# Expert stages of a two-layer network: weights in longer runs, the next pair's gather inside this pair's chain, the overflow branch at the end

## The chip, the cores and the metric

The kernel runs on one core of one Trainium2 chip. The metric is device time in microseconds (us) of one execution, taken as the median of the runs.

## What is computed

A stack of two blocks over 256 tokens of 1024 features, all in float32. The first block (two layers of a feed-forward net, three attention branches and another feed-forward net) is not touched. The second block has two layers; each is a mixer (a state space mixer in layer 0, dilated attention in layer 1), a layer norm, a mixture of experts, and a layer norm:

```python
g_w, g_idx = lax.top_k(softmax(xf @ w_rg + b_rg), 1)        # one of 4 groups
e_w, e_idx = lax.top_k(softmax(e_logits of that group), 2)  # two of its 8 experts
gates = g_w * e_w / sum(e_w)
# every expert's tokens, in blocks:
h = silu(xb @ w_gate[e]) * (xb @ w_up[e])                   # 1024 -> 512
y = h @ w_down[e]                                           # 512 -> 1024
x = layer_norm(ALPHA * x + sum over a token's experts of gate * y)
```

There are 32 experts; each one's three matrices hold 2 MiB each, so a layer reads 192 MiB of expert weights.

## The kernel before

**Shape of an expert stage.** `moe` works on x with features on partitions (X["h"] and X["l"], its high and low parts, and X["T"], the sum of both). The router multiplies x with the router's weights (L1302, L1303), turns the logits over to tokens (L1308) and picks experts on VectorE. Meanwhile x is turned to tokens on partitions (L1349, evicted by ScalarE into `xt`, L1350). A product of masks with a triangle gives each token's place in its experts' lists (L1355 to L1359), `rk`.

**A pair.** The 32 experts are worked off as 16 pairs, 64 places to an expert, so that a pair fills 128 columns. `pair(q)` asks for the pair's twelve tiles of weights (`load`, each 1 MiB: four of w_gate, four of w_up, four of w_down), builds the one-hot matrices of places (`ot`, L1580) and the same with the tokens' weights (`ogt`, L1587), and calls `run`. In `run` TensorE does in this order:

1. the gather: `xg` = the pair's tokens as columns, 16 products of 128x128 (L1455) into two PSUM tiles of 512 columns, each copied to SBUF by VectorE (L1460);
2. two transposes of `ogt` (L1463), evicted by ScalarE to `og` (L1465);
3. the gate and up products (L1478) into `gps` and `ups`; ScalarE then makes tanh of `gps` (L188), VectorE two steps to `t` (L1493, L1494);
4. four transposes of `t` into `htp` (L1497), copied by VectorE to `hT` (L1499);
5. the down products (L1510) into two `yp`, evicted by ScalarE to `y` (L1519);
6. eight products of `y` with `og` (L1535), summed over all pairs in `eacc`, four PSUM tiles.

The float32 products are two TensorE instructions each. The stationary side of the gate, up and down products is 64 columns wide, the two experts of the pair side by side; that of the others is 128 wide. The small PSUM tiles (`xgp`, `ogp`, `htp`, `yp`) all come from one pool with two buffers, `mp`, in turn.

In the first pair the term ALPHA * x is added to `eacc` as 16 products of `xt` with a scaled identity (`residual`, L1437), tied behind the gate products. In the last pair `run` also makes the mean of the sum for the layer norm that follows.

**Weights.** SyncE issues the loads. The tiles lie in 21 slots that are used in a fixed turn (`ORDER`, `next_tile`), so the loads run ahead of TensorE by at most that many. Each load sends row `c * 128 + p` of a stretch of the matrix to partition p, column group c:

```python
t = next_tile([128, 4, HID])
x = nc.sync.dma_start(out=t, in_=w[k][h * 512:(h + 1) * 512, :].rearrange("(c p) m -> p c m", p=128))
```

so a contiguous run is one row: 2 KB of w_gate and w_up, 4 KB of w_down.

**Overflow.** An expert may have more than 64 tokens. `beyond` (after pair 1) counts the blocks beyond the first; `more` (after pair 10, `MOREQ`) reads that number into a register of each engine and holds a branch (L1594) around a loop that treats one block a turn. Its body asks for six weight slots of its own, so the turn of slots moves on by six there. With the inputs used the number is zero: the branch is taken past the loop.

The order on each engine is made by a scheduler from the program's order, its dependencies and some ties written by hand.

Of the kernel before, what the change touches and what calls it, by code (L numbers as in the profile page):

```python
# [10 lines left out]
F32 = mybir.dt.float32  # L11
# [7 lines left out]
D = 1024  # L19
S = 256  # L20
KC = D // 128
# [10 lines left out]
W1 = 0  # L32
W2 = 4
# [14 lines left out]
def tile_stack(ctx: ExitStack, tc: tile.TileContext, a: dict, out: bass.AP):  # L48
# [20 lines left out]
    def after_norm(*ins):  # L69
        """no split but the first few between the operations of a layer norm."""  # L70
# [119 lines left out]
    def table(name):  # L190
        """the functions' tables, loaded behind the last tanh."""
# [4 lines left out]
    def warm(out, n, after):  # L196
        """the array's clock falls in a pause: idle products, into a sum not in use, keep it up."""
# [5 lines left out]
    def last_chunks(accs, ks, first):  # L203
        """the products of the last chunks, (wh, wl, mh, ml) each, into one output chunk."""
# [113 lines left out]
    def ffn(l, w1, w2, g, b, setup=None):  # L318
        with pool(name="accps", bufs=1, space=PSUM) as aps, pool(name="gups", bufs=2, space=PSUM) as gps, \
# [26 lines left out]
            def gate_up(js):  # L346
                """the hidden chunks js; features outermost, so that it can start on the first of them."""
# [42 lines left out]
    def log1p_exp_neg_abs(pool, x, shape, tag):  # L390
        """log(1 + exp(-|x|)) by the series of atanh."""
# [34 lines left out]
    def bias_tile(pool, h, queue=None, bufs=3):  # L426
        """T[q, k] = rel[bucket(128 + q - k), h], with the mask of the head's kind."""
# [48 lines left out]
    def token_mix(l):  # L476
        w_in, w_gate, w_out = a["w_in"][l], a["w_gate"][l], a["w_out"][l]
        with ExitStack() as st:
# [25 lines left out]
            def split_pair(t0, t1, c0):  # L504
                """stationary columns: 64 of t0, 64 of t1."""
# [19 lines left out]
            def k_pad(ps, kz, i):  # L525
                """a projected pair of keys into two tiles, each with zeros in the other's rows."""
# [10 lines left out]
            def v_tok(ps, v, i):  # L537
                """keys on partitions: v[:, tile, i, :]."""
# [7 lines left out]
            # compressed keys and values  # L546
# [28 lines left out]
            def compress(i, ts):  # L575
                """four products side by side, then their sum."""
# [26 lines left out]
            # compressed keys  # L603
# [23 lines left out]
            # compressed values  # L627
# [15 lines left out]
            # gates of the three branches and the forget gate  # L643
# [15 lines left out]
            # the running sums of the forget gates  # L659
# [9 lines left out]
            # attention over the compressed blocks, all heads at once  # L669
# [29 lines left out]
            def attend(q, kz, bias, sink=None, gate=None):  # L699
                """probabilities of one head, keys on partitions: [k0 x (q0 q1) | k1 x q1]."""  # L700
# [27 lines left out]
            def pv(po, jobs):  # L728
                """jobs[g]: list of (v of tile 0, v of tile 1 or None, probabilities)."""
# [55 lines left out]
            # NSA  # L785
# [17 lines left out]
            # sliding window with sinks  # L803
# [20 lines left out]
            # forgetting attention  # L824
# [79 lines left out]
    def rsqrt_tile(pool, v, eps, n=S):  # L904
        """(v + eps) ** -0.5, refined by a step of Newton's."""
# [9 lines left out]
    def ssd(g, b):  # L915
        w_in, w_out = a["ssd_w_in_2"][0], a["ssd_w_out_2"][0]
        with ExitStack() as st:
# [13 lines left out]
            def conv(ps, c, dst):  # L931
                """causal convolution of four taps, then twice its silu."""
# [9 lines left out]
            # the keys and queries of the states, B and C  # L942
# [6 lines left out]
            # steps, decays and their running sums  # L949
# [47 lines left out]
            def mix(j, xs, csb, y):  # L997
                """the states' sums for two heads."""
# [115 lines left out]
            # sin, with its sign by row, and cos, one where nothing turns  # L1114
# [136 lines left out]
    NE, CAP, HID, NOV = 32, 64, 512, 7  # L1251
    AHEAD = 7
    MOREQ = 10
# [18 lines left out]
    def router_parts(rp, l):  # L1272
        """the router's weights, high and low parts side by side."""
# [5 lines left out]
    def moe(l, g_, b_, rs, write=False):  # L1279
        w_g, w_u, w_d = a["moe_w_gate_2"][l], a["moe_w_up_2"][l], a["moe_w_down_2"][l]  # L1280
        with ExitStack() as st:
# [27 lines left out]
            warm(accs[0][:, 0, :], W1, x)  # L1309
            # the groups' logits, filled up to eight, then the experts'  # L1310
# [7 lines left out]
            def top(x, name):  # L1318
                """the eight highest logits in order, and where they stand."""
# [8 lines left out]
            # the experts of the other groups far below  # L1328
# [8 lines left out]
            # which experts  # L1337
# [22 lines left out]
            warm(accs[0][:, 0, :], W2, x)  # L1360
# [367 lines left out]
```

## Time and profile before

| | |
|---|---|
| median of 3 runs | 2939.51 us (2937.55 to 2939.96) |
| span of the profiled execution, first to last instruction | 2939.3 us |
| TensorE (products) busy | 2802.7 us, 95% of the span |
| TensorE's weight loads | 2199.8 us, 75% |
| VectorE | 1421.7 us, 48% |
| ScalarE | 1050.9 us, 36% |
| GpSimd | 196.5 us, 7% |
| mean granted TensorE clock | 0.988 |
| moved by DMA | 697.44 MB, mean 237 GB/s |

The profile gives each instruction's start and length, and for each idle stretch the event that ended it. Products are pipelined on TensorE: a row's length includes the way through the array, so rows overlap, and the step between two starts is what one costs. The expert stage of layer 0 runs from about 1684 to 2204 us, that of layer 1 from about 2405 us to the end.

### The profile page before, as it was taken

The page shows a single profiled execution, that of the slowest core. Times are in us where ns is not written, and L with a number is a line of the kernel's source. Part 1 is how long each engine was busy: PE and PEld are TensorE (multiplying, and loading weights), DVE is VectorE, ACT ScalarE, POOL GpSimd, SP SyncE. Part 2 cuts the span into 40 slices and gives each one's busy share as a digit, 9 for nine tenths or more (in the row PEclk, how much of TensorE's full clock was granted, in tenths as well). Part 3 has the DMA queues.
Part 4 walks back from the last instruction along what each step waited for, and adds up shares of the span by engine and source line. Part 5 has one row for each costly group of instructions (what it writes and reads, how often), then busy time and mean ns, then how long its engine had stood idle before and what let it go on. Part 6 is the DMA issues. An engine that isn't in the chain of part 4 may idle for free. (4 is left out here: it accounts for less than half of the span.)

```text
span 2939.3 us, 46679 instructions
## 1 busy us (share of the span) xinstructions
PE 2802.7 (95%) x19161; PEld 2199.8 (75%) x19161; DVE 1421.7 (48%) x3075; ACT 1050.9 (36%) x1949; POOL 196.5 (7%) x263
## 2 busy tenths in 40 slices
PE   8899999999999999999999999999998989999998
PEld 8798899999999889999989854454448974444454
DVE  5466665755655765665688731111127762111113
ACT  4344555544544454544477510000015530000002
POOL 2102000200201100020100100000001010000000
PEclk9899999999999999999999999999999999999999
DMA  8666454455454745445455699998985479999896
GB/s 223 193 201 158 126 159 138 156 184 185 149 194 137 186 130 167 153 139 193 131 194 180 229 364 393 395 393 323 393 305 169 137 256 356 394 393 393 300 394 230
DMA packets 426793, 697.44 MB, mean 237 GB/s; under 512 B 19460, under 2 KB 238384, under 8 KB 426576
## 3 DMA queue, kind: packets, MB, share of 16 engines
q1 hardware_dynamic: 414976, 677.62, 66.3%
q10 hardware_dynamic: 9296, 11.66, 1.3%
q0 software_dynamic: 2304, 5.15, 1.2%
q8 instruction: 152, 2.49, 0.4%
q14 instruction: 65, 0.53, 0.1%
HBM read 693.25 MB, written 4.27 MB: 237 GB/s over the span
## 5 line engine op out<-in xcount | busy, mean ns | idle before, releaser
L84 DVE TENSOR_TENSOR whl<-w,whl 128x1024 fp32r<-128x1024 f32 x487 | 591.5, 1220 | 349.2 <-ACT whl L83 344.2
L83 ACT ACTIVATE whl<-w 128x1024 fp32r<-128x1024 f32 x487 | 507.3, 1050 | 355.9 <-PE gu L113 105.8
L111 PE MATMUL pp<-xh,whl 128*128 128x256 f32 x1432 | 418.1, 292 | 9.0 <-ACT xh L307 4.0
L112 PE MATMUL pp<-xl,whl 128*128 128x256 f32 x1432 | 418.7, 292 | 1.0 <-DVE xl L308 1.0
L113 PE MATMUL pp<-xh,whl 128*128 128x256 f32 x1432 | 412.8, 288 | 0.4 <-DVE whl L510 0.4
L111 PE MATMUL gu<-xh,whl 128*128 128x256 f32 x1408 | 401.6, 286 | 9.9 <-DVE h L361 7.2
L113 PE MATMUL gu<-xh,whl 128*128 128x256 f32 x1408 | 401.4, 285 | 0.5 <-DVE whl L84 0.5
L112 PE MATMUL gu<-xl,whl 128*128 128x256 f32 x1408 | 401.6, 285 | 0.0
L111 PEld LDWEIGHTS pp<-xh,whl 128*128 128x128 f32 x1432 | 274.6, 192 | 17.4 <-ACT xh L307 5.7
L112 PEld LDWEIGHTS pp<-xl,whl 128*128 128x128 f32 x1432 | 275.0, 192 | 10.0 <-issue 6.9
L111 PEld LDWEIGHTS gu<-xh,whl 128*128 128x128 f32 x1408 | 272.8, 194 | 12.2 <-ACT whl L83 9.4
L113 PEld LDWEIGHTS pp<-xh,whl 128*128 128x128 f32 x1432 | 274.6, 192 | 4.3 <-issue 2.4
L112 PEld LDWEIGHTS gu<-xl,whl 128*128 128x128 f32 x1408 | 273.0, 194 | 0.8 <-DVE xl L308 0.7
L113 PEld LDWEIGHTS gu<-xh,whl 128*128 128x128 f32 x1408 | 272.9, 194 | 0.8 <-DVE whl L84 0.8
L1460 DVE COPY xg<-xgp 128x512 f32<-128x512 f32 x60 | 41.5, 692 | 358.5 <-PE xgp L1455 358.5
L111 PE MATMUL acc<-hhi,whl 128*128 128x256 f32 x704 | 201.7, 287 | 2.4 <-DVE rT L231 2.2
L112 PE MATMUL acc<-hlo,whl 128*128 128x256 f32 x704 | 200.1, 284 | 0.0
L113 PE MATMUL acc<-hhi,whl 128*128 128x256 f32 x704 | 199.1, 284 | 0.0
L1493 DVE SCALAR_TENSOR_TENSOR t<-t,gps 128x512 f32<-128x512 f32 x32 | 22.0, 688 | 324.4 <-ACT t L188 324.4
L1519 ACT ACTIVATE y<-yp 128x512 f32<-128x512 f32 x60 | 35.8, 597 | 347.7 <-PE yp L1510 347.7
L111 PEld LDWEIGHTS acc<-hhi,whl 128*128 128x128 f32 x704 | 135.8, 193 | 5.4 <-DVE rT L231 4.0
L112 PEld LDWEIGHTS acc<-hlo,whl 128*128 128x128 f32 x704 | 135.8, 193 | 0.2
(571 smaller groups left out, 5063.0 us busy)
## 6 DMA issues: line engine op xcount, KB each, us to landing
w<-in_ffn_w_dram SPq DMA_DIRECT2D x130, 1024.0 KB, 5.3
wa<-in_moe_w_up_dram SPq DMA_DIRECT2D x48, 1024.0 KB, 14.2
whl<-in_moe_w_down_dram SPq DMA_DIRECT2D x47, 1024.0 KB, 14.1
wa<-in_moe_w_gate_dram SPq DMA_DIRECT2D x43, 1024.0 KB, 14.2
whl<-in_moe_w_gate_dram SPq DMA_DIRECT2D x39, 1024.0 KB, 14.1
wa<-in_moe_w_down_dram SPq DMA_DIRECT2D x37, 1024.0 KB, 13.4
whl<-in_moe_w_up_dram SPq DMA_DIRECT2D x36, 1024.0 KB, 14.2
w<-in_moe_w_down_dram SPq DMA_DIRECT2D x32, 1024.0 KB, 14.4
```

The costliest lines, as they stand in the source:

```text
L83: after_norm(nc.scalar.activation(out=hi, in_=w, func=AF.Copy), nc.vector.tensor_tensor(out=lo, in0=w, in1=hi.bitcast(F32), op=ALU.subtract))
L84: nc.vector.tensor_tensor(out=lo, in0=w, in1=hi.bitcast(F32), op=ALU.subtract))
L111: nc.tensor.matmul(out=o, lhsT=wh, rhs=xh, start=first, stop=False, skip_group_check=skip)
L112: nc.tensor.matmul(out=o, lhsT=wh, rhs=xl, start=False, stop=False, skip_group_check=skip)
L113: return nc.tensor.matmul(out=o, lhsT=wl, rhs=xh, start=False, stop=last, skip_group_check=skip)
L1460: nc.vector.tensor_copy(out=xg[:, q * 4:q * 4 + 4, 0:P], in_=ps[:, :, 0:P])
L1493: nc.vector.scalar_tensor_tensor(out=t[0:P], in0=t[0:P], scalar=1.0, in1=gps[0:P], op0=ALU.add, op1=ALU.mult)
L1519: nc.scalar.activation(out=y[0:P, hs], in_=yp[0:P], func=AF.Copy)
```

## The change

Six things, all in `moe`:

- the loads give each partition consecutive rows: four rows of w_gate or w_up (8 KB), two of w_down (8 KB). To match, `xt` is written with its features in another order (the eviction reads PSUM with a step of four elements), and the transposes of `t` read every second column;
- `run` gets a finished `xg`. The gather of the next pair is split in halves: the first goes behind the gate and up products, the second behind the transposes of `t`. The first half's copy is ScalarE's, the second's VectorE's. `ot` of the next pair is built before `run`;
- `phase` ties every group of TensorE instructions behind the group before it;
- `y` takes the room of `t` and `hT`, and `xg` has its own;
- ALPHA * x is eight products of the scaled identity with X["T"] (256 columns each), put between the router's products; the idle products after L1359 write another PSUM tile;
- `more` moves from behind pair 10 to before the last pair, behind that pair's loads.

```diff
-    MOREQ = 10
+            def residual(c):
+                nc.tensor.matmul(out=accs[c // 2][:, c % 2, :], lhsT=alphas, rhs=X["T"][:, c, :], start=(c % 2 == 0), stop=False,
+                                 skip_group_check=True)
             for c in range(KC):
...
+                if c >= 2:
+                    residual(c - 2)
...
-            warm(accs[0][:, 0, :], W1, x)
+            for c in (KC - 2, KC - 1):
+                residual(c)
...
-                    nc.scalar.activation(out=xt[:, i, q * 512:(q + 1) * 512], in_=pt.rearrange("p c t -> p (c t)"), func=AF.Copy)
+                    nc.scalar.activation(out=xt[:, i, q * 512:(q + 1) * 512].rearrange("p (k f) -> p k f", k=4),
+                                         in_=pt.rearrange("p c t -> p (c t)").rearrange("p (f k) -> p k f", k=4), func=AF.Copy)
...
+            def phase(*ins):
+                for x in ins:
+                    if done.get("pe") is not None:
+                        tc.add_manual_dep(x.ins, done["pe"].ins.name, order, reason="phase")
+                done["pe"] = ins[-1]
+
+            def gather(os, P, xg):
+                def half(q):
+                    ps = mp.tile([128, 4, 128], F32, tag="m", name="xgp")
+                    first = "r" not in done
...
+                    phase(*ms)
+                    if not first:
+                        first_copy(1 - q)(out=xg[:, q * 4:q * 4 + 4, 0:P], in_=ps[:, :, 0:P])
+                return [lambda q=q: half(q) for q in range(2)]
...
                 tanh(out=t[0:P], in_=gps[0:P], scale=0.5)
+                if then:
+                    then.pop(0)()
...
-                    nc.tensor.transpose(ht[:, c, 0:P], t[0:P, c * 128:(c + 1) * 128], ident[0:P, 0:P])
+                phase(*[nc.tensor.transpose(ht[:, c, 0:P], t[0:P, c // 2 * 256 + c % 2:(c // 2 + 1) * 256:2], ident[0:P, 0:P])
+                        for c in range(4)])
                 nc.vector.tensor_copy(out=hT[:, :, 0:P], in_=ht[:, :, 0:P])
+                if then:
+                    then.pop(0)()
...
-                residual()
...
-                            x = nc.sync.dma_start(out=t, in_=w[k][h * 512:(h + 1) * 512, :].rearrange("(c p) m -> p c m", p=128))
+                            x = nc.sync.dma_start(out=t, in_=w[k][h * 512:(h + 1) * 512, :].rearrange("(p c) m -> p c m", p=128))
...
-                        nc.sync.dma_start(out=t, in_=w[2][h * 256:(h + 1) * 256, :].rearrange("(c p) m -> p c m", p=128))
+                        nc.sync.dma_start(out=t, in_=w[2][h * 256:(h + 1) * 256, :].rearrange("(p c) m -> p c m", p=128))
...
+            for q in range(NP):
+                ld = load([(w_g[e], w_u[e], w_d[e]) for e in (2 * q, 2 * q + 1)])
+                if q == 0:
+                    os = places(0)
+                    weights()
+                    xg, steps = gather_pair(os)
+                    for f in steps:
+                        f()
+                if q == NP - 1:
+                    more()
+                ogs = weighted(q, os)
+                steps = ()
+                if q < NP - 1:
+                    os = places(q + 1)
+                    hold = {}
+
+                    def first_half(os=os, hold=hold):
+                        hold["xg"], hold["steps"] = gather_pair(os)
+                        hold["steps"][0]()
+
+                    steps = (first_half, lambda hold=hold: hold["steps"][1]())
+                last = run(xg, ogs, ld, 2, q == NP - 1, steps)
```

The body of `more`'s loop takes a seventh slot, for its own `xg`.

## Rows read from the trace of the kernel before

**Rows 1.** The page: TensorE's and VectorE's shares, and GB/s in 40 slices.

```profile
PE 2802.7 (95%) x19161; PEld 2199.8 (75%) x19161; DVE 1421.7 (48%) x3075; ACT 1050.9 (36%) x1949; POOL 196.5 (7%) x263
GB/s 223 193 201 158 126 159 138 156 184 185 149 194 137 186 130 167 153 139 193 131 194 180 229 364 393 395 393 323 393 305 169 137 256 356 394 393 393 300 394 230
```

**Rows 2.** TensorE's waits, 1700 to 2200: total us, times, longest.

```profile
PE htp L1497 <- DVE t L1494: 13.5, 15, 0.9
PE yp L1510 <- DVE hT L1499: 11.0, 14, 0.8
```

**Rows 3.** Timeline, one pair: start, length, instruction, count [idle before <- releaser].

```profile
1840.99 3.60 PE L1478 MATMUL ups<-whl,xg 128*64 128x512 f32 x16
...
1845.50 0.63 PE L1497 MATMUL htp<-ident,t 128*128 128x128 f32 x4 [0.91 <-DVE t L1494]
1846.16 0.69 DVE L1499 COPY hT<-htp 128x512 f32<-128x512 f32 x1 [0.81 <-PE htp L1497]
1846.91 0.64 PE L1510 MATMUL yp<-whl,hT 128*64 128x512 f32 x1 [0.78 <-DVE hT L1499]
...
1853.93 3.72 PE L1535 MATMUL eacc<-og,y 128*128 128x256 f32 x16
...
1857.48 3.73 PE L1455 MATMUL xgp<-ot,xtok 128*128 128x128 f32 x32
...
1861.06 0.38 PE L1463 MATMUL ogp<-ident,ogt 128*128 128x128 f32 x2
```

**Rows 4.** Timeline of TensorE, the first pair of layer 0.

```profile
1715.83 4.02 PE L1478 MATMUL ups<-wa,xg 128*64 128x512 f32 x15
1719.78 1.16 PE L1437 MATMUL eacc<-alphas,xtok 128*128 128x128 f32 x8
1720.77 0.60 PE L1497 MATMUL htp<-ident,t 128*128 128x128 f32 x4
1721.21 1.06 PE L1437 MATMUL eacc<-alphas,xtok 128*128 128x128 f32 x8
1722.20 7.09 PE L1510 MATMUL yp<-whl,hT 128*64 128x512 f32 x32
```

**Rows 5.** Router of layer 0: waits, then GpSimd's writes of X["T"], then timeline.

```profile
PE lgp L1302 <- ACT xh L307: 2.1, 3, 0.8
...
L310 POOL TENSOR_SCALAR xT<-rT,pars x8: 917/1059/1456, 1683.6 to 1691.7; 128x256 f32<-128x256 f32 x8
...
1692.87 4.08 PE L1349 MATMUL xtp<-ident,xT 128*128 128x128 f32 x16
1696.89 0.41 PE L1355 MATMUL rkp<-mk,tri 128*128 128x32 f32 x2
1696.99 0.60 ACT L1350 ACTIVATE xtok<-xtp 128x512 f32<-128x512 f32 x1 [0.26 <-PE xtp L1349]
1699.85 1.05 PE L1455 MATMUL xgp<-ot,xtok 128*128 128x128 f32 x8
```

**Rows 6.** Around the branch: SyncE's longest wait, VectorE's and TensorE's first work behind it.

```profile
SPq L1564 <- PE gps L1478: 22.6, 1, 22.6
...
2042.39 0.49 DVE L1587 TENSOR_TENSOR ogt<-ot,gt 128x128 f32<-128x128 f32 x2 [9.84 <-PEq L1594]
2042.56 1.69 PE L1455 MATMUL xgp<-ot,xtok 128*128 128x128 f32 x13 [0.30 <-PEq L1594]
```

**Rows 7.** Stretches: busy us (instructions) by engine, clock, DMA share, GB/s.

```profile
1884.00:1887.00 3.00, 3.00 (x15) 2.08 (x12) 0.00 (x0) 0.60 (x1) 0.00 (x0) 1.00 1.04 385
1908.00:1911.00 3.00, 2.63 (x13) 0.92 (x15) 0.32 (x1) 0.00 (x0) 0.00 (x0) 1.00 1.02 409
2000.00:2020.00 20.00, 19.31 (x106) 11.28 (x108) 2.02 (x3) 1.58 (x3) 0.00 (x0) 1.00 0.39 156
2180.00:2182.00 2.00, 2.00 (x12) 0.62 (x10) 0.00 (x0) 0.18 (x1) 0.00 (x0) 1.00 0.52 207
```

**Rows 8.** Timeline, last pair of layer 0: the first product that reads the last weights.

```profile
2191.05 0.59 PE L1510 MATMUL yp<-whl,hT 128*64 128x512 f32 x1
```

More of the change, by code (lines that the diff above doesn't have):

```diff
@@ L1429, in beyond @@
                     nc.vector.tensor_tensor(out=rkb[:, i, 0:NOV], in0=rkb[:, i, 0:NOV], in1=base, op=ALU.subtract)
-            def residual():
-                if "r" not in done:
-                    done["r"] = True
-                    for c in range(KC):
-                        for i in range(2):
-                            x = nc.tensor.matmul(out=accs[c // 2][:, c % 2, i * 128:(i + 1) * 128], lhsT=xt[:, i, c * 128:(c + 1) * 128],
-                                                 rhs=alphas, start=(c % 2 == 0 and i == 0), stop=False, skip_group_check=True)
-                            tc.add_manual_dep(x.ins, done["up"].ins.name, order, reason="gates first")
             done = {}
@@ L1444, in first_copy @@
                 return nc.vector.tensor_copy if k == 0 else (lambda out, in_: nc.scalar.activation(out=out, in_=in_, func=AF.Copy))
-            def run(os, ogs, loads, n, last):
+            def phase(*ins):
[7 more added lines that the diff above has]
+                    first = "r" not in done
+                    ms = []
+                    for c in range(4):
+                        for i in range(2):
+                            ms.append(nc.tensor.matmul(out=ps[:, c, 0:P], lhsT=xt[:, i, (q * 4 + c) * 128:(q * 4 + c + 1) * 128], rhs=os[i],
+                                                       start=(i == 0), stop=(i == 1)))
+                        if first:
+                            first_copy(c % 2)(out=xg[:, q * 4 + c, 0:P], in_=ps[:, c, 0:P])
+                    phase(*ms)
+                    if not first:
+                        first_copy(1 - q)(out=xg[:, q * 4:q * 4 + 4, 0:P], in_=ps[:, :, 0:P])
+                return [lambda q=q: half(q) for q in range(2)]
@@ L1448, in run @@
+            def run(xg, ogs, loads, n, last, then=()):
                 P = n * CAP
                 wg, wu, wd = loads
-                xg = wk.tile([128, KC, 128], F32, tag="xy", name="xg", bufs=1)
-                for q in range(2):
-                    ps = mp.tile([128, 4, 128], F32, tag="m", name="xgp")
-                    for c in range(4):
-                        for i in range(2):
-                            nc.tensor.matmul(out=ps[:, c, 0:P], lhsT=xt[:, i, (q * 4 + c) * 128:(q * 4 + c + 1) * 128], rhs=os[i],
-                                             start=(i == 0), stop=(i == 1))
-                        if "r" not in done:
-                            first_copy(c % 2)(out=xg[:, q * 4 + c, 0:P], in_=ps[:, c, 0:P])
-                    if "r" in done:
-                        nc.vector.tensor_copy(out=xg[:, q * 4:q * 4 + 4, 0:P], in_=ps[:, :, 0:P])
+                then = list(then)
@@ L1516, in run @@
                     nc.vector.reduce_sum(out=ysum[:, 1:2], in_=yps[1], axis=AX.X)
+                if not last:
+                    ys = [wk.tile([128, 512], F32, tag=k, name="y", bufs=1) for k in ("t", "hT")]
                 for hf, yp in enumerate(yps):
                     hs = slice(hf * 512, (hf + 1) * 512)
-                    nc.scalar.activation(out=y[0:P, hs], in_=yp[0:P], func=AF.Copy)
+                    nc.scalar.activation(out=y[0:P, hs] if last else ys[hf][0:P], in_=yp[0:P], func=AF.Copy)
                     if last:
@@ L1582, in pair, with weighted @@
                     os.append(o)
-                if q == 0:
-                    weights()
+                return os
+            def weighted(q, os):
+                ogs = []
                 for i, o in enumerate(os):
@@ L1605, in more @@
                             ogs.append(og)
-                        run(os, ogs, ld, 1, False)
-            for q in range(NE // 2):
-                last = pair(q)
+                        xg = next_tile([128, KC, 256])
+                        done["pe"] = None
+                        for f in gather(os, CAP, xg):
+                            f()
+                        run(xg, ogs, ld, 1, False)
+                        done["pe"] = None
+            NP = NE // 2
+            for q in range(NP):
[5 more added lines that the diff above has]
+                    for f in steps:
+                        f()
+                if q == NP - 1:
[10 more added lines that the diff above has]
+                last = run(xg, ogs, ld, 2, q == NP - 1, steps)
+                if q < NP - 1:
+                    xg = hold["xg"]
                 if q == 1:
                     beyond()
-                if q == MOREQ:
-                    more()
             st4.close()
```

44 lines of the change are left out of this document (22 added, 22 removed).

## The prediction

> **What bounds the kernel now.** I read the page first. TensorE is busy for 95% of the span, VectorE for half; in the expert stages (slices 24 to 30 and 33 to 39 of the GB/s line) the transfers run at 393 to 395 GB/s, where other stages need 130 to 250 [rows 1]. So there are two candidates in the stages that the change touches: TensorE's chain, or the weights. The waits decide it. Over the 16 pairs of layer 0 TensorE waits 13.5 us for `t` before the transposes and 11.0 us for `hT` before the down products, and no wait for a transfer is among the long ones [rows 2]. The weights are in time, though they stream at a rate that looks like a ceiling. Then one pair in the timeline, to see what its steps cost [rows 3]. The gate and up products step by 0.43 us for two instructions side by side, so a group of 16 takes 3.44 us and TensorE is free again at 1840.99 + 3.44 = 1844.43. The down products start at 1846.91. These 2.48 us hold four transposes (0.63 with the way through the array) and two pauses of 0.91 and 0.78, each a round trip over VectorE. The gather costs 1861.06 - 1857.48 = 3.58, 0.112 an instruction. One pair, from one gather to the next, is 4 x 3.44 + 2.48 + 7.02 (down) + 3.55 (`eacc`) + 3.58 + 0.31 (transposes of `ogt`, with the change to half-width products) = 30.7 us. Twelve loads of 1 MiB in that time are 410 GB/s, a little more than the loads reach, so the lead that they have shrinks as the stage goes on.
>
> **Gather between the phases.** This is the main term. Before, a pair pays 2.48 + 3.58 = 6.06 us for the pauses, the transposes and the gather. After, the gather's halves lie in the pauses. What they meet there is shown by the first pair, where eight residual products already fill each pause [rows 4]: the `ups` end their last step at 1715.83 + 9 x 0.43 = 1719.70, the filling starts 0.08 later, the transposes 0.10 after eight instructions, and they take 0.44; the down products follow eight more instructions after another 0.10. A half gather is 16 instructions, 1.79 us, so `t` (wanted at 1844.43 + 1.07 in [rows 3]) and `hT` (0.75 after the transposes) are both there before the half is done. New is a wait on PSUM. `mp` has two buffers and the turn is `ogp`, half 1, `htp`, half 2, `yp`, `yp`: half 2 needs half 1's buffer, so ScalarE's copy must be done. The nearest row is ScalarE's eviction of `xt`, the same shape, 0.60 us [rows 5]. With 0.16 until the last product is out of the array (0.275 long, stepping by 0.112), 0.03 to start the copy and 0.06 to release TensorE (both as at `hT`, [rows 3]) that is 0.85 after half 1's last step, of which the transposes cover 0.54; 0.31 us stays. Half 2's copy (VectorE, 0.69) is over 0.94 after its end, before the second `yp` starts 0.10 + 1.72 after it: nothing. So after: 0.09 + 1.79 + 0.85 + 1.79 + 0.10 = 4.62 us, 1.44 less a pair. Bounds: without the PSUM wait 1.75 less; with the copy held up by another 0.8 us in ScalarE's queue, about 0.6 less. I take 1.44, since ScalarE has nothing else to do there (tanh is long done). Fourteen pairs a layer: 20.2 us.
>
> The first pair has its pauses filled already, so there the gain is the residual leaving: 1722.20 - 1719.70 = 2.50, plus the other 16 of the residual's 32 instructions, which came elsewhere in the pair (16 x 0.112 = 1.79) and the next gather (3.58) is 7.87, against 4.62: 3.2 us. The last pair has no successor and keeps its pauses; its own gather has moved into pair 14 at the price counted there.
>
> **Residual in the router.** Eight products of 256 columns are what the eight products into `eacc` are, 3.6 us [rows 3]. TensorE idles 2.1 us in three pauses of the router for `xh` alone [rows 5], and there are smaller ones. X["T"] comes from GpSimd at about 1.13 us a chunk, from 1683.6 on [rows 5], the last about at 1692.7; the product that wants a chunk comes two chunks behind the router's and the last two come behind the transposes of the logits, next to those of x, which read X["T"] from 1692.87 on without a pause. So I take it as not late. What the pauses do not take delays the turning of x (16 instructions in 4.08 us) and with it L1355, which started as that ended [rows 5]. I take 0.7 us a layer. Bounds: nothing, and 2.5 us if the products step at the slow pace that the router's neighbours have there (0.255 an instruction for L1349 against 0.112 for the same width in a gather).
>
> **The reordered features.** The transposes of `t` read every second column. No row shows a strided read, but were a transpose twice as long, 0.44 us more would mostly lie in the 0.31 us that TensorE waits for the copy anyway. The evictions of `xt` read PSUM with a step of four; they take 0.60 us each, the last ends at 1697.59, and the first gather starts 2.3 us later, behind other work [rows 5]. Both nothing. [...]
>
> **The branch moved.** At pair 10 the body's six slots are skipped, so the next loads wait 22.6 us for TensorE to free theirs [rows 6], and the transfers run at a share of 0.39 in 2000 to 2020, against 1.04: 12.5 us of transfer are lost [rows 7]. TensorE never felt that, so it is worth nothing by itself; it is cover, used below. At its new place nothing of the stage is queued behind it on SyncE. On VectorE, `ogt` of the last pair is: VectorE waited 9.84 us for TensorE to pass the branch, then made two `ogt` in 0.49 [rows 6]. Before, TensorE had a gather to do meanwhile and lost 0.30; now the transposes of `ogt` are first in the fixed order, so it waits for one `ogt` too: half of 0.49, and two handovers of some 0.1 more. 0.5 us a layer.
>
> **Weights in 8 KB runs.** In stretches where w_gate and w_up land (2 KB runs) 385 GB/s are moved, where w_down lands (4 KB) 409 [rows 7]. I expect 409 or a little more for everything, some 17 us less transfer a layer. TensorE does not wait for weights, so this is worth nothing; the cover that it could need is worked out here. The last weights of layer 0 land about at 2181, when the share falls to 0.52 [rows 7], and are read at 2191.05 [rows 8]: 10 us to spare. TensorE will want them 22 us earlier; the transfers are 12.5 us earlier without the skipped slots. At the old rate that is just enough, at the new one ample.
>
> **Sum.** A layer: 20.2 + 3.2 - 0.7 - 0.5 = 22.2; two: 44.4 us. The profiled execution's span is 2939.3, 0.2 below the median of the runs. 2939.5 - 44.4 = 2895 us.
>
> **Rivals.**
> 1. *The order costs what it fills.* The fixed order with two PSUM buffers makes each copy a wait: if half 2 waits for a copy that is 0.8 us later than I think, a pair gains 0.6, the first pair 2.4, and with 1.3 us lost in router and branch a layer gains 9.5: 2920 us. For it: every handover then lies on TensorE's path. Against: the first pair of before runs this very pattern with 0.1 us a handover [rows 4].
> 2. *No PSUM wait*: 1.75 a pair, 3.6 in the first: 27 a layer, 2886 us.
> 3. *The runs stay as they are* (the two sides of the transfer are not joined to one run): the rate stays at 385 and 409, and the last weights land at 2181 - 12.5 = 2168.5 when they are wanted at 2168.8. Then the last pair waits up to 3 us: 2895 to 2901.
> 4. *Slower: the wider pitch costs transfer rate.* The loads would then end the stage. The stream from 1700 to 2181 is 481 us, 468.5 without the hole; it may reach until 2191 before the stage is longer than before, so this decides from a rate 4.8% lower on. At 10% lower it is 24 us more a layer than before: 2988 us. Against it: going from rows of 2 KB to rows of 4 KB raised the rate [rows 7]. [...]
>
> **Chances.** The forecast 0.67 (2885 to 2907), rival 1 0.12, rival 2 0.08, rival 3 0.07, rival 4 0.05; 0.01 for something else. A change of 0.2%, 6 us, is about what a measurement of this kernel tells from none. Faster by more: all but rival 4 and a bad case of rival 1, 0.93; the same 0.02; slower 0.05. The range leaves out rival 4 and the ends of rivals 1 and 2: 2882 to 2920.
>
> **What the profile after would show.** Right: a pair of 29.3 us instead of 30.7; no pause before the transposes or the down products in pairs 1 to 14; one of about 0.3 us before half 2, ended by ScalarE's copy; no L1437 in the first pair; no hole in the transfers two thirds into a stage; 8 KB packets and over 400 GB/s throughout, later on falling to TensorE's need. Wrong: waits for transfers on TensorE (rivals 3 and 4), longer waits for `xgp` copies (rival 1), a router that ends over 1 us later, or a handover at the branch of several us.

## The result, and the profile after

The changed kernel takes 2909.22 us (median of 4 runs, 2905.07 to 2913.70) against 2938.53 (4 runs, 2937.38 to 2939.96) for the kernel before on the same chip: ratio 0.9898, 95% interval [0.9884, 0.9912], 29.3 us faster. The profiled execution took 2909.27, its span is 2907.4. The forecast was 2895: the right direction, inside a range that reaches up to rival 1's 2920, with a third of the gain missing. Most of what is missing, 6.6 us a layer, lies at the start of each expert stage; the 2.9 us that pairs 1 to 14 gained less than forecast is largely made up by 2.1 in the last pair.

The page of the changed kernel, for [rows 1]:

```profile
PE 2806.7 (97%) x19129; PEld 2194.8 (75%) x19129; DVE 1402.8 (48%) x3051; ACT 1069.7 (37%) x1985; POOL 196.1 (7%) x263
...
GB/s 225 194 203 149 134 154 145 145 194 189 155 179 161 179 118 163 145 147 191 167 133 192 220 309 416 421 421 421 421 230 181 132 232 328 421 421 421 421 421 98
DMA packets 312106, 697.45 MB, mean 240 GB/s; under 512 B 19460, under 2 KB 238384, under 8 KB 262736
```

The transfers now run at 421 GB/s through both stages, without the hole, and 49 thousand packets hold 8 KB or more. TensorE's waits from 1700 to 2190, for [rows 2]:

```profile
PE xgp L1459 <- ACT xg L1442: 4.4, 18, 0.4
PE xgp L1459 <- DVE xg L1462: 3.4, 8, 0.5
...
PE ogp L1475 <- DVE ogt L1608: 0.9, 1, 0.9
PE yp L1527 <- issue: 0.8, 1, 0.8
...
PE htp L1512 <- DVE t L1510: 0.3, 1, 0.3
```

The 24.5 us for `t` and `hT` are gone but for 1.1 in the last pair (the rows of `yp` and `htp`); what is new is waits for copies of `xg`. Line 1462 is VectorE's share of the chunk copies, made only in the first two gathers of a layer: eight waits of up to 0.5 us. One pair from the middle, timeline, for [rows 3]:

```profile
1815.72 2.05 PE L1459 MATMUL xgp<-ot,xtok 128*128 128x128 f32 x16
1815.86 0.69 DVE L1510 TENSOR_TENSOR t<-t,ups 128x512 f32<-128x512 f32 x1 [2.06 <-PE ups L1491]
1817.61 0.64 PE L1512 MATMUL htp<-ident,t 128*128 128x128 f32 x4
1817.81 0.60 ACT L1442 ACTIVATE xg<-xgp 128x512 f32<-128x512 f32 x1 [4.72 <-PE xgp L1459]
1818.28 0.69 DVE L1515 COPY hT<-htp 128x512 f32<-128x512 f32 x1 [1.74 <-PE htp L1512]
1818.46 2.05 PE L1459 MATMUL xgp<-ot,xtok 128*128 128x128 f32 x16 [0.21 <-ACT xg L1442]
...
1820.44 4.08 PE L1527 MATMUL yp<-w,hT 128*64 128x512 f32 x17
...
1845.21 1.05 PE L1459 MATMUL xgp<-ot,xtok 128*128 128x128 f32 x7
```

This is the pattern that was forecast: no pause before the transposes or the down products, and one of 0.21 before half 2, ended by ScalarE's copy. The pair takes 1845.21 - 1815.72 = 29.49. The start of pair 1's gather, inside pair 0, looks different; TensorE's timeline:

```profile
1723.52 0.71 PE L1459 MATMUL xgp<-ot,xtok 128*128 128x128 f32 x4
1724.62 0.71 PE L1459 MATMUL xgp<-ot,xtok 128*128 128x128 f32 x4 [0.38 <-DVE xg L1462]
1725.74 0.71 PE L1459 MATMUL xgp<-ot,xtok 128*128 128x128 f32 x4 [0.42 <-ACT xg L1442]
1726.91 0.71 PE L1459 MATMUL xgp<-ot,xtok 128*128 128x128 f32 x4 [0.45 <-DVE xg L1462]
1727.46 0.64 PE L1512 MATMUL htp<-ident,t 128*128 128x128 f32 x4
```

Here a half takes 3.94 us instead of 1.89, because every four products wait for the copy of the four before. Laid out by stage, layer 0, from the starts of the first instructions in the timelines (us; a pair is counted from its `ogp` to the next one's, and the column "whole copies" is the kernel of the first experiment):

| stretch | before | changed | whole copies | change forecast |
|---|---|---|---|---|
| first router product to first rank product | 12.83 | 14.36 | 14.37 | +0.7 |
| to the first gather | 2.95 | 2.92 | 2.92 | 0 |
| first gather to `ogp` | 5.68 | 7.60 | 3.57 | 0 |
| pair 0 | 32.61 | 33.21 | 29.54 | -3.2 |
| pairs 1 to 14, sum | 431.2 | 414.4 | 414.4 | -20.2 + 0.5 |
| last pair to `ymp` | 27.20 | 25.12 | 25.13 | 0 |
| all | 512.5 | 497.6 | 490.0 | -22.2 |

### The profile page after: what moved, and what is told of

Read it like the earlier page. It is cut to its first block, busy times and chain, and to the rows that moved or that the text cites. A ratio compares the mean times of both kernels' runs of the same rounds, so it can differ in the third digit from the quotient of the medians.

```text
span 2907.4 us, 46673 instructions
## 1 busy us (share of the span) xinstructions
PE 2806.7 (97%) x19129; PEld 2194.8 (75%) x19129; DVE 1402.8 (48%) x3051; ACT 1069.7 (37%) x1985; POOL 196.1 (7%) x263
## 5 line engine op out<-in xcount | busy, mean ns | idle before, releaser
L1459 PEld LDWEIGHTS xgp<-ot,xtok 128*128 128x128 f32 x1024 | 120.9, 191 | 50.3 <-issue 24.3
L1459 PE MATMUL xgp<-ot,xtok 128*128 128x128 f32 x1024 | 136.9, 283 | 15.8 <-ACT xg L1442 9.0
L187 ACT ACTIVATE t<-gps 128x512 f32<-128x512 f32 x32 | 19.1, 597 | 320.8 <-PE gps L1491 320.8
```

Source lines behind the costliest of these rows:

```text
L187: last_tanh.append(nc.scalar.activation(out=out, in_=in_, func=AF.Tanh, **kw))
L1459: ms.append(nc.tensor.matmul(out=ps[:, c, 0:P], lhsT=xt[:, i, (q * 4 + c) * 128:(q * 4 + c + 1) * 128], rhs=os[i], start=(i == 0), stop=(i ...
```

## The experiments

Unless said otherwise each starts from the changed kernel; the diffs are shortened. The kernel before lies between 2935 and 2944 us in all of them.

**Whole copies.** The chunk copies of the first two gathers become half copies.

```
-                    first = "r" not in done
+                    first = False
```

> The changed kernel, but the gathers of the first two pairs are copied out of PSUM half by half, as all later ones are, and not feature chunk by feature chunk. Nothing is left out of the computation. Theory A (the missing part of the gain lies in the first two gathers of each layer, where every four products wait 0.37 to 0.45 us for the copy of the four before): the gather of pair 0 takes about 4.5 us instead of 7.6, the two halves of pair 1's gather about 1.9 us each instead of 3.9 and 4.0, so 3 + 4 = about 7 us a layer less, of which up to 1 us comes back where pair 0's gates wait for the whole copy of the second half: 2895 to 2899 us against 2909. Rival (the chunk copies only show up there; the products of the first pairs are late for another reason, the vector engine's work for the routing weights and the overflow blocks): the waits move to another releaser, within 3 us of the changed kernel, 2906 to 2912 us.

Measured: 2894.16 us, ratio 0.9827 [0.9813, 0.9840], 15 us faster than the changed kernel's first measurement. The first gather, timeline:

```profile
1698.81 3.73 PE L1459 MATMUL xgp<-ot,xtok 128*128 128x128 f32 x32
...
1702.38 0.38 PE L1475 MATMUL ogp<-ident,ogt 128*128 128x128 f32 x2
```

3.57 us instead of 7.60, and pair 0 takes 29.54 instead of 33.21: 7.7 us in layer 0, as theory A says, and nothing comes back.

**The residual elsewhere in the router.**

```
-                if c >= 2:
-                    residual(c - 2)
...
-            for c in (KC - 2, KC - 1):
+            for c in range(4):
                 residual(c)
...
-            warm(gup.tile([128, HID], F32, tag="u", name="idle")[:, 0:256], W2, x)
+            for c in range(4, KC):
+                y = residual(c)
+                tc.add_manual_dep(y.ins, x.ins.name, order, reason="behind the ranks")
```

> The changed kernel, but the eight residual products stand elsewhere: four behind the router's logits and their transposes, four behind the rank products in the place of the four idle products there. Nothing is left out of the computation. Theory B (the residual products hold up the logits because they wait 2 us for GpSimd's xT between the router's products): from the first logit product to the first rank product 12.8 to 13.4 us instead of 14.36, and from there to the first gather at most 3.5 us instead of 2.92: 0.5 to 1 us a layer less, 2907 to 2908 us against 2909. Rival (their own time on TensorE, 5.6 us a layer, is what costs, wherever they stand in the router): logits to gather stays at 17.3 us within 0.3 and the time at 2909 us.

Measured: 2910.04 us, 0.9887 [0.9872, 0.9903]. It decides nothing: the first four products were placed between the router's products again, and the granted clock fell. A stretch of its layer 0 (us, busy us of PE, PEld, DVE, ACT, POOL, clock, DMA share, GB/s):

```profile
1692.00:1696.00 4.00, 3.68 (x18) 3.07 (x16) 2.42 (x20) 1.84 (x4) 0.00 (x0) 0.50 0.97 410
```

Logits to ranks fell to 12.55 us, but ranks to first gather rose to 5.68 and the gather to 8.35. Four residual products now stand before the gather, and the clock is 0.50 in 1696 to 1700 and 0.77 in 1700 to 1704, around its start at 1699.71.

**No residual.** From the kernel with whole copies, without the two calls of `residual` in the router; the first pair's combine starts the sums, and ALPHA * x is missing from them.

> The kernel with whole half copies (2894 us) without the residual products in the router; the first pair's combine starts the sums. Left out of the computation: x times alpha in the sum. Theory B2 (in the router the eight residual products cost the 1.5 us by which the first rank product came later): logits to first rank product 12.8 us instead of 14.4, 3 us for both layers: 2889 to 2892 us. Rival B3 (they also keep TensorE busy enough there that the granted clock stays at 1.00, as it did not in the kernel before, 0.50 to 0.88 between logits and gather; without them the transposes, the ranks and the first gather run at the lower clock): logits to rank 12.5 to 13 us, but 1 to 3 us of it given back up to the first gates: 2893 to 2899 us.

Measured: 2889.03 us, 0.9827 [0.9814, 0.9841]. Logits to ranks 12.83 and 12.72 us, which is what the kernel before needs; ranks to gather 2.97 and 2.92. So in the router the residual costs 1.53 us a layer. That rests on the stretches: the time by itself does not show 3 us, for the ratio is that of the kernel with whole copies, 0.9827 both times. The router of layer 0:

```profile
1688.00:1692.00 4.00, 3.58 (x16) 2.98 (x17) 3.11 (x26) 2.15 (x6) 0.31 (x1) 0.50 0.99 406
1692.00:1696.00 4.00, 4.00 (x26) 3.48 (x25) 3.05 (x20) 1.03 (x3) 0.00 (x0) 0.91 0.98 399
```

The clock fell as the rival says, yet the 12.8 us hold even so, and up to the first gates nothing was given back.

**The runs back.** Loads, copies of the tokens and slices of the hidden features as before.

```
-    rearrange("(p c) m -> p c m", p=128)
+    rearrange("(c p) m -> p c m", p=128)
...
-    t[0:P, c // 2 * 256 + c % 2:(c // 2 + 1) * 256:2]
+    t[0:P, c * 128:(c + 1) * 128]
```

> The changed kernel with the weights loaded in the order of the kernel before (runs of 2 KB for gates and ups, 4 KB for downs), and with the plain copies of the tokens and the plain slices of the hidden features that go with it; the phases, the gather's place, the residual and the branch as changed. Nothing is left out. Theory C (the transfers are hidden at either rate, because the last weights land long before they are used): 2905 to 2913 us, no different from the changed kernel, with the expert stage's rate back at 385 to 394 GB/s. Rival D (pairs of 29.5 us use the weights faster than 387 GB/s can bring them, 12.58 MB in 29.5 us being 426 GB/s): TensorE waits for transfers in the second half of each layer; 16 pairs of 12.58 MB at 390 GB/s are 516 us a layer less the start of the loads ahead of the stage (some 35 us of transfers), against 497.6 us from the first logit to the end of the changed kernel's stage, so up to 10 us a layer: 2915 to 2930 us.

Measured: 2909.84 us, 0.9894 [0.9879, 0.9909]: no different. A stretch of it:

```profile
2000.00:2020.00 20.00, 20.00 (x96) 8.79 (x94) 1.18 (x3) 2.18 (x4) 0.00 (x0) 1.00 1.04 398
```

TensorE waits for no transfer. But it is close. The last load of the stage (its issue, then the time from issue to landing) and the first product that reads it:

```profile
L1589 SPq DMA_DIRECT2D w<-in_moe_w_down_dram x1: 1369/1369/1369, 2158.5 to 2158.5; - x1
DMA to landing us min/median/max: 16.6/16.6/16.6
```

```profile
2176.35 3.63 PE L1526 MATMUL yp<-w,hT 128*64 128x512 f32 x16
```

It lands near 2175, some 1.3 us before its use. In the changed kernel the last load is issued at 2133.7 and lands 13.3 us later, 30 us before its use at 2177.14. The long runs buy cover, not time.

**The long runs alone**, in the kernel before. Its residual reads the tokens by chunk, so the gather takes its columns at the new stride.

```
-    lhsT=xt[:, i, (q * 4 + c) * 128:(q * 4 + c + 1) * 128], rhs=os[i],
+    lhsT=xt[:, i, q * 512 + c:(q + 1) * 512:4], rhs=os[i],
```

> The kernel before with the weights in runs of 8 KB and nothing else of the change: the products of the gather and of the hidden transposes take their stationary columns at the strides that the new order of features asks for (every fourth, every second). Nothing is left out of the computation. Theory C (hidden transfers): 2935 to 2942 us, as the kernel before (2938.5), with the rate of the expert stage up from 385-394 to about 420 GB/s and a longer quiet stretch of the queues at the end of each layer. Rival (the kernel before is held up by its transfers somewhere): 3 us or more faster than 2938.5. A third way (reading stationary columns at a stride costs the weight loads of the gather): the 32 weight loads of a gather longer than 130 ns each and the pair longer than 30.8 us, so up to 2950 us.

Measured: 3071.01 us, 1.0445 [1.0431, 1.0460]. The third way, and far more than its bound. The weight loads by line, first this kernel, 1750 to 2150, then the kernel before:

```profile
L1455 PEld LDWEIGHTS xgp<-ot,xtok 128*128 128x128 f32 x352 | 83.0, 329 | 0.9 <-issue 0.7
```

```profile
L1455 PEld LDWEIGHTS xgp<-ot,xtok 128*128 128x128 f32 x416 | 48.4, 192 | 1.3 <-issue 0.7
```

329 ns instead of 192, and the step of a gather's product follows (TensorE is busy 0.24 us with each instruction instead of 0.12: 82.9 us for 352, 48.6 for 416); most pairs take 34.6 us instead of 30.7. Some take 36.3, with longer down products (those from `whl` 635 ns instead of 596); why is open. The run says nothing on the transfers, but it prices what the change avoids by reordering the tokens in ScalarE's copy.

**The branch back** behind pair 10.

```
-                if q == NP - 1:
-                    more()
...
+                if q == 10:
+                    more()
```

> The changed kernel with the branch over the overflow blocks behind pair 10, as before, and not ahead of the last pair. Nothing is left out. Theory (the branch costs 0.5 to 1.1 us wherever it stands; the transfers have cover for it at both places): pair 14 back from 30.6 to 29.5 us, pair 10 or 11 0.5 to 1.5 us longer, total within 2 us of the changed kernel (2909). Rival (with pairs of 29.5 us the transfers that the branch holds up are missed later in the layer): a wait of TensorE for a transfer in pairs 11 to 15 of several us, 2912 us or more.

Measured: 2915.41 us (2910.86 to 2919.18), 0.9912 [0.9895, 0.9928]. Inside the stage: pair 14 takes 29.54 instead of 30.60, pair 10 30.28 instead of 29.54, and the last pair 26.49 instead of 25.13. The hole is back (share 0.39 in 2000 to 2020) and no transfer is missed. So the branch itself costs 0.74 or 1.06 us, and the place at the end gains 1.36 in the last pair. The rest of this run's time is the second layer's, whose first gather and pair 0 are together 4.5 us longer than the changed kernel's; the granted clock is 0.50 to 0.92 from 2406 to 2426. Measured again, the changed kernel took 2916.04 (below), so the times show no difference between the two places. The last pair here and in the changed kernel, TensorE's timeline:

```profile
2159.40 0.70 PE L1501 MATMUL meanp<-room,ones 128*128 128x256 f32 x2
...
2171.46 0.72 PE L1512 MATMUL htp<-ident,t 128*128 128x128 f32 x4 [0.91 <-DVE t L1510]
```

```profile
2171.18 0.70 PE L1501 MATMUL meanp<-room,ones 128*128 128x256 f32 x2
2172.14 0.72 PE L1512 MATMUL htp<-ident,t 128*128 128x128 f32 x4 [0.25 <-DVE t L1510]
```

With the branch ahead of this pair VectorE's sums come late, so the mean's product no longer stands between the gates: it fills the pause for `t`.

**No fixed order.**

```
-                    if done.get("pe") is not None:
+                    if False:
```

> The changed kernel without the fixed order of phases: the gather is still written between this pair's products, the chunk copies of the first two gathers are still there, but TensorE's instructions are tied to nothing and the program's own scheduler places them. Nothing is left out of the computation. Theory A2 (the chunk copies stood in the kernel before too, and cost little there because other products could run while one chunk was copied; the order of phases shut these out): products of gates stand between those of the first gather again, gather and pair 0 together 37.3 to 38.5 us a layer instead of 40.8, the middle pairs within 0.3 us of 29.5, the last pair back at 27.2 from 25.1 because the mean's product stands ahead of the gates again: about 2905 to 2909 us. Rival (the chunk copies stall TensorE in any order): gather and pair 0 stay at 40.8 us, and the time is 2909 us or more.

Measured: 2942.56 us, 1.0012 [1.0002, 1.0022]: the whole gain is gone. Theory A2 holds for the first gather alone: 5.84 us in layer 1, against 7.74 with the order and 5.82 in the kernel before. Pair 0 takes 34.19, and since it draws in products of pair 1, which takes 28.63, it stays at 33.3 when these are put back. The last pair stays at 25.11. What decides had not been foreseen: from pair 6 on a pair takes 31.5 us. TensorE's timeline of one:

```profile
1953.45 0.71 PE L1459 MATMUL xgp<-ot,xtok 128*128 128x128 f32 x4
1954.09 1.07 PE L1491 MATMUL ups<-whl,xg 128*64 128x512 f32 x2
1955.10 1.60 PE L1459 MATMUL xgp<-ot,xtok 128*128 128x128 f32 x12
...
1968.02 0.72 PE L1512 MATMUL htp<-ident,t 128*128 128x128 f32 x4 [0.87 <-DVE t L1510]
```

Left to itself, the scheduler puts half 1 among the gates and ups, where nothing waits, and the pause for `t` is back. In pairs 2 to 4 it had put it where the order does, at 29.49 us; why it changes is open.

**The gather at the end** of its pair, in the kernel with whole copies and the fixed order.

```
-                if then:
-                    then.pop(0)()
...
                 phase(*[combine(c) for c in range(KC)])
+                for f in then:
+                    f()
```

> The kernel with whole half copies (2894 us) and the fixed order of phases, but the next pair's gather stands behind this pair's combine and not between its products. Nothing is left out. Main theory (the gather pays as the work that fills the two waits of the pair, for the hidden features and for their transposes, and takes its own copies off the path): waits of 0.9 and 0.8 us back at the transposes and at the down products, pairs of 30.6 to 31.2 us instead of 29.5, 15 pairs in two layers, so 33 to 50 us more: 2927 to 2944 us. Rival 1 (the order of phases by itself or the whole copies made the gain): pairs below 30 us, within 10 us of 2894.

Measured: 2941.28 us, 1.0002 [0.9990, 1.0014]. Most middle pairs take 30.82 to 30.87 us (pairs 9 and 14 some 2 us more), and both pauses are back; the waits from 1750 to 2150:

```profile
PE htp L1510 <- DVE t L1508: 10.9, 12, 0.9
PE yp L1523 <- DVE hT L1513: 10.2, 13, 0.8
```

It is 47 us against the kernel with whole copies: the place of the gather is the whole gain, and the order of phases is what holds it there.

**Split copies**, in the kernel with whole copies.

```
-                        first_copy(1 - q)(out=xg[:, q * 4:q * 4 + 4, 0:P], in_=ps[:, :, 0:P])
+                        for k in range(2):
+                            first_copy(k)(out=xg[:, q * 4 + k * 2:q * 4 + k * 2 + 2, 0:P], in_=ps[:, k * 2:k * 2 + 2, 0:P])
```

> The kernel with whole half copies (2894 us), and besides each half of a gather copied out of PSUM by VectorE and ScalarE at once, two chunks each. Nothing is left out. Theory E (the 0.2 us that the second half of each gather waits for ScalarE's copy of the first, 0.60 us long, is the last wait in the pair that the copies cause): 0.2 us a pair less, 29.3 instead of 29.5, so 5 to 6 us: 2888 to 2890 us. Rival (VectorE's share of the copy stands in front of the hidden features' product with the ups or of their copy, and puts the same wait there): pairs of 29.4 to 29.7 us and 2892 to 2898 us.

Measured: 2897.91 us, 0.9855 [0.9839, 0.9872]; pairs of 29.74 us instead of 29.49. Timeline:

```profile
1839.48 0.42 DVE L1466 COPY xg<-xgp 128x256 f32<-128x256 f32 x1 [1.26 <-PE xgp L1459]
1839.94 0.38 ACT L1442 ACTIVATE xg<-xgp 128x256 f32<-128x256 f32 x1 [5.18 <-DVE xg L1466]
1839.97 0.69 DVE L1516 COPY hT<-htp 128x512 f32<-128x512 f32 x1
1840.38 2.05 PE L1459 MATMUL xgp<-ot,xtok 128*128 128x128 f32 x16 [0.45 <-ACT xg L1442]
```

ScalarE waits until VectorE has left the buffer: 0.42 and 0.38 one behind the other take longer than 0.60 at once. The rival is right: the wait before half 2 grows from 0.21 to 0.45.

**The changed kernel again**, unchanged.

> The changed kernel as it is, on the chip of the runs beside it. Theory F (its runs spread over 5 to 9 us, because TensorE's granted clock falls in the router of a layer in some executions and not in others, and the stretch that follows, gather of pair 0 and gather of pair 1 with their waits, is then run at the lower clock): the runs lie between 2903 and 2914 us, and the longer ones have the lower mean granted clock. Rival (the spread comes from the transfers or from the start of the kernel): no relation of time and mean clock.

Measured: 2916.04 us, 0.9918 [0.9905, 0.9932]: one run of 2907.23 with a mean granted clock of 0.991, four of 2914.41 to 2917.35 with 0.988 or 0.989. Beside the kernel before it is 24 us faster here, against 29 at first. The longer runs have the lower clock, as theory F says, but they lie above its 2914. In the kernel with whole copies likewise: 2886.9 and 2887.3 at 0.993, 2894.2 to 2895.2 at 0.991. The place is seen where a profile caught it, in layer 1 of that kernel:

```profile
2392.00:2396.00 4.00, 3.08 (x18) 2.60 (x17) 2.99 (x22) 0.91 (x3) 0.00 (x0) 0.82 0.82 270
2396.00:2400.00 4.00, 4.00 (x25) 3.55 (x24) 2.32 (x13) 0.00 (x0) 0.00 (x0) 0.75 0.77 324
```

There ranks to gather took 4.58 us instead of 2.92. That every long run lost its time there is not shown.

**Two additions to the kernel with whole copies**: the last pair's weighted places ahead of the branch, and then three idle products behind the transposes of the logits as well.

```
+                ogs = weighted(q, os)
                 if q == NP - 1:
                     more()
-                ogs = weighted(q, os)
```

```
+            idle = gup.tile([128, HID], F32, tag="u", name="idle")[:, 0:256]
+            warm(idle, 3, x)
```

> The kernel with whole half copies (2894 us), and the weighted places of the last pair computed ahead of the branch over the overflow blocks, in place of behind it (the branch's own weighted places get a buffer of their own). Nothing is left out of the computation. Theory G (of the 1.06 us by which the pair ahead of the branch is longer, 0.90 is TensorE's wait for these weighted places and nothing else stands behind it): 0.8 to 1.1 us a layer less, 2892 to 2893 us. Rival (TensorE itself waits at the branch as long): pair 14 stays at 30.6 us, 2894 us.

> As the kernel with the weighted places ahead of the branch, with three idle products more, behind the transposes of the logits in the router. Nothing is left out of the computation. Theory F (the granted clock falls in the router in some executions for want of work on TensorE): the clock stays at 1.00 through router and first gather in both layers, and the runs spread by less than 5 us around 2891 to 2894 us. Rival (three products of 0.25 us are too few to matter, or stand in the way of the ranks): the same spread as without, or 0.3 to 0.7 us a layer more.

Measured: 2894.03 us, 0.9845 [0.9831, 0.9858], and 2889.79, 0.9834 [0.9819, 0.9848]. Pair 14 falls from 30.60 to 30.00; TensorE's own passing of the branch is left, a wait of 0.3:

```profile
PE ogp L1475 <- PEq L1618: 0.3, 1, 0.3
```

That is 1.2 us in all, too little for the runs to tell. With the idle products the clock was 1.00 in both routers of the profile and the ranks came no later than 0.2 us, but the runs still spread over 7 us (2887.52 to 2894.60), as they do without, where theory F had less than 5; so the router's clock is not shown to make the spread. The two intervals overlap. This last kernel has the lowest median of the complete ones, 26 us below the changed kernel beside it; by its ratio, 0.9834, it is not told from the kernel with whole copies, 0.9827.

## Why the prediction was right, and where it failed

**Gather between the phases: right, 0.2 us a pair too much.** A pair was to gain 1.44 us; 30.73 less 29.49 is 1.24. The handovers were as worked out: half 2 starts 0.85 us after half 1's last step, which ends where the transposes start. Each half took 1.89 instead of 1.79, which makes the 0.2 us a pair, 2.8 a layer. Gather at the end and no fixed order show that this term is the gain: take away either and 2941 to 2943 us are back.

**The first pair: the step that failed.** I gave pair 0 the 4.62 us of the others and so 3.2 us of gain; it lost 0.6, and the first gather, for which I counted nothing, lost 1.9. The chunk copies now apply until pair 0 has ended, so to pair 1's gather too, which the kernel before copies by halves; that costs pair 0 3.7 us, 33.21 against 29.54 with whole copies, and stays without the order of phases (33.3). In the first gather the order costs: nothing may stand between a chunk and its copy. In the kernel before VectorE's first two chunk copies come together, and TensorE makes 16 instructions behind them without a wait (timeline):

```profile
1700.94 0.48 DVE L1458 COPY xg<-xgp 128x128 f32<-128x128 f32 x2
1701.28 2.24 PE L1455 MATMUL xgp<-ot,xtok 128*128 128x128 f32 x16 [0.38 <-DVE xg L1458]
```

Even chunks go to VectorE and odd ones to ScalarE, so these two are chunk 0 of either half: the halves alternated, each in its own buffer, and one was filled while the other was copied. The order of phases ends that; without it the first gather is back at 5.84 us. In the changed kernel only the step from half 1 to half 2, that is to the other buffer, is without a wait, inside this row of the first gather:

```profile
1705.00 1.16 PE L1459 MATMUL xgp<-ot,xtok 128*128 128x128 f32 x8 [0.45 <-DVE xg L1462]
```

The chunks of a half have places of their own in its buffer, and still products wait 0.37 to 0.45 us for the copy of another chunk of their half; and in the split copies ScalarE starts its copy at 1839.94, 0.04 us after the end of VectorE's, although the two only read the buffer, and different chunks of it. Whether the program or the chip asks for these waits is not shown. With whole copies pair 0 gains 3.07, the 3.2 of the forecast, and the kernel is at 2894. Its sum, 22.5 us less in layer 0, meets the forecast 22.2 in part by errors that cancel: router and pairs gave less, first gather and last pair more.

**Residual in the router: mis-sized.** 1.53 us a layer, forecast 0.7, and so a router over 1 us later, which the prediction names as a sign of being wrong. "Not late" was wrong: TensorE waits for GpSimd's xT in five places before the logits are complete. The program writes each residual product two chunks behind the router's, but nothing ties it there, and the first stands right behind the first router product:

```profile
PE eacc L1301 <- POOL xT L309: 1.9, 5, 0.6
```

```profile
1685.09 0.70 PE L1301 MATMUL eacc<-xT,alphas 128*128 128x256 f32 x2 [0.30 <-POOL xT L309]
1685.44 0.47 PE L1306 MATMUL lgp<-xl,rs 128*36 128x256 f32 x1
```

The router's next products stand behind it. The kernel without the residual has all of the 1.53 back.

**The branch moved: the right size, and one thing overlooked.** Pair 14 is 1.06 longer, and pair 10 keeps what the branch cost it in the kernel before, 0.55 (31.33 beside pairs of 30.78; the prediction's 0.30 was TensorE's own wait): 0.5 net, as forecast. Not foreseen were the 1.36 that the last pair gains because the mean's product falls into its pause. The other 0.7 of the 2.08 there shows in the last pair of the kernel before:

```profile
2176.55 1.02 PE L1478 MATMUL gps<-w,xg 128*64 128x512 f32 x2
...
2181.19 4.02 PE L1478 MATMUL ups<-w,xg 128*64 128x512 f32 x15
```

At the ends of this stretch four instructions go one at a time, 0.43 us each, where elsewhere two go side by side: 0.86 us more, of which the down products make up a little. The order of phases keeps them in twos, 16 in 3.60.

**Weights in 8 KB runs and reordered features: right.** No time either way, and the cover is ample. The rate did not fall to TensorE's need, for a pair of 29.49 us needs 427 GB/s. The strided copy of `xt` takes 591 ns against 597. The strided transposes do cost something, as these weight loads of the changed kernel and of the runs back, with plain slices, show (ns, least, median, most):

```profile
L1512 PEld LDWEIGHTS htp<-ident,t x128: 194/207/219, 1727.3 to 2876.5; 128*128 128x128 f32 x128
```

```profile
L1511 PEld LDWEIGHTS htp<-ident,t x128: 138/141/144, 1726.6 to 2876.5; 128*128 128x128 f32 x128
```

Four transposes take 0.64 us for the 0.60 of [rows 4], and as forecast that goes into the wait for half 1's copy: the pairs take 29.49 either way. So a weight load of every second f32 took 207 ns here for 141, and one of every fourth 329 for 192 in the long runs alone; ScalarE's copy, which reads PSUM at every fourth, shows no loss. Whether the long runs are worth time at 2890 us was not tried; the last products come some 7 us sooner in the stage there, and the short runs had 1.3 us to spare.

Of the rivals, the first named what happened, but in the wrong place: a handover that costs what it fills, in the first two gathers only. Rivals 3 and 4 fell with the 421 GB/s. Rival 4's price takes a transfer that is 10% longer for a rate that is 10% lower; such a rate makes 468.5 us into 521, 30 us a layer more and not 24. Nothing hangs on it. That a wider pitch costs rate, by a tenth or at all, no run shows: with 8 KB from one partition's rows to the next one's, stretches moved 418 to 423 GB/s, more than the 385 and 409 with 2 and 4 KB [rows 7].

## What to carry to other kernels

When an order of work is fixed by hand, look for the places where the old free order hid a handover, above all in the first and last turn of a loop, where special cases live. A fine-grained copy that let the next step start early became a stall here, 0.37 to 0.45 us at a chunk, where copy and products share a PSUM buffer and nothing else may stand between them. Work placed in a pause needs something that keeps it there: without the order the same program gained nothing.

## What the runs showed of the hardware

The clock that TensorE was granted in the router differed from profile to profile, also where the router is written the same. In 1692 to 1696 it was 0.50 in the kernel before, 1.00 in the changed one, where the residual products stand between the router's, and 0.50 again when four of these were moved. In the second layer, whose router is written the same, it stayed at 1.00 in the changed kernel's profile and fell to 0.57 between ranks and gather (2406 to 2410) in that of the branch back. Within a kernel, runs that differ by 8 us, 0.3%, differ by 0.002 to 0.003 in mean clock.

Stretches with runs of 8 KB moved 418 to 423 GB/s, against 385 with 2 KB and 409 with 4 KB [rows 7].
